# Down products of two MLPs by seven block products in place of eight, and a first projection that takes the weighted input

## The chip, the cores and the metric

The kernel runs on one core of a Trainium2 chip as a single program. Its engines work side by side, each through its own list of instructions in a fixed order: TensorE (PE, matmuls, with weight loads listed as PEld), VectorE (DVE), ScalarE (ACT), GpSimd (POOL) and SyncE (SP), which here issues most DMAs. They wait for one another by semaphores. The metric is the device time of one execution in microseconds.

## The reference

Two transformer blocks are computed on x of 1024 positions and 1024 features, in float32. Both end in the same kind of MLP, with 4096 inner features:

```
# block 1
u = rmsnorm(h, norm_mix);  proj = u @ w_in
h = h + concat(attention(proj), gated_deltanet(proj)) @ w_o
m = rmsnorm(h, norm_mlp)
h = h + square(relu(m @ w_up)) @ w_down
gate = sigmoid(rmsnorm(h, norm_ple) @ w_ple_gate)
h = h + gate * (p @ w_ple_proj)
x = rmsnorm(h, norm_final)
# block 2
u = rms_norm(x, norm_mix_2) @ w_in_2
x = x + concat(pool_mixer(u), hgrn2(u)) @ w_out_2
x = x + square(relu(rms_norm(x, norm_mlp_2) @ w_up_2)) @ w_down_2
return rms_norm(x, norm_final_2)
```

Attention is causal with a sliding window of 128 and rotary positions; the gated delta net and HGRN2 are recurrences over chunks of 64.

## The kernel before, in words

Activations are kept transposed: a tile holds 128 features by 512 positions (a half, h = 0 or 1). To keep float32 accuracy each operand is split into a high and a low part: a cast on ScalarE makes the high part (L203), a subtraction the low one (L204, mostly on VectorE). A product takes three matmuls per block of 128x128 weights: high by high (L223), high by low (L224), low by high (L225). Weight tiles are 128x1024; their parts are called wh and wl, those of activations u.

*The up product of an MLP* is done as a 2x2 block matrix product (feature tiles by halves) by seven block products in place of eight, after Strassen and Winograd. The operands made of the activations (b11, b21, and t1, t2, t3, b22, t4) are formed once, in the norm before it. For each of 16 pairs of inner feature tiles, n, the weight is read as four 128x512 tiles a11, a12, a21, a22 (L974, 256 KB each). Sums of these (s1 and s2 at L1006, L1007; two more at L1016, L1017) are split, and the products t2, t1, t3, b22, t4 follow, 12 matmuls each. VectorE adds each product to the running sums s and q as it ends (L1010, L1014, L1021, L1022, L1026, L1030). The products with b11 and b21 belong to the function `first`. For the first 12 n (HP) they are done ahead of the loop, from whole 512 KB tiles, and the partial sum goes through DRAM (p1s); for the last four they stand within the loop. A finished inner tile passes relu and square (L963, L964) and is put into the DRAM tensor `hid` (L965).

*The down product* is plain: for each half h and each half c4 of the output features four PSUM banks are filled over 8 groups g. A group takes two weight tiles of 512 KB and four tiles of `hid`, each split into high and low, and issues 48 matmuls. At the end of such a pass VectorE adds the four banks to the residual (L1055). Between the halves, `between` enters the norm of the first half of the result, to be worked off in small steps beside the matmuls (`tick`).

*The first projection* of block 1 (w_in) has two kinds of input. The attention's part takes xg, x times the norm's gain, and its results are multiplied by the reciprocal root Rs; the delta net's part takes u, x scaled fully (L281) and split. The rotary products run on GpSimd.

*What sets the order.* The kernel is written in a tile framework. It gives each engine one static order, by a scheduling of the whole program in which a tile is given its buffer when it is first written, and the buffers of one name come round in program order. In the up loop weight tiles and the results of sums draw their buffers from five such rings (x, y0, y1, y2, z) in a fixed sequence (`tq`). SP issues its DMAs in its static order: one that waits holds up those behind it.

Of the kernel before, what the change touches and what calls it, by code (L numbers as in the profile page):

```python
# [61 lines left out]
def block_kernel(ctx: ExitStack, tc: tile.TileContext, A):  # L62
# [186 lines left out]
    def rms(x, eps, r=None):  # L249


        a = tt("ac")
        SC.activation(a, x[0], ACTF.Square)
        for k in range(1, KD):
            sq = tt("sq")
            if r is not None and k % 2:
                G.tensor_tensor(sq, x[k], x[k], ALU.mult)
            else:
                SC.activation(sq, x[k], ACTF.Square)  # L259
            V.tensor_tensor(a, a, sq, ALU.add)  # L260
# [243 lines left out]
    res, hid = dram.tile([D, S], F32, name="res"), dram.tile([4 * D, S], F32, name="hid")  # L504
# [7 lines left out]
    xx, xg, u, Rs = [[], []], [[], []], [None, None], [None, None]  # L512
    r8 = const.tile([128, NC], F32, name="r8")

    def start(h):
        for k in range(KD):
            t = th(h, k)
            nc.sync.dma_start(out=t, in_=A["xT"][cs(k), hs(h)])
            xx[h].append(t)
            if h == 0 and k == KD - 1:  # L520
                early.append(load_w(A["w_in"][17]))
        for k in range(KD):
            hi, lo, g = tu(), tu(), small("norm_mix", k)
            SC.activation(hi, xx[h][k], ACTF.Copy, scale=g)
            V.scalar_tensor_tensor(lo, xx[h][k], g, hi.bitcast(F32), ALU.mult, ALU.subtract)
            xg[h].append((hi, lo))
        Rs[h] = td("b", 1 + h)
        SC.copy(Rs[h], value(rms(xx[h], 1e-6, r8[:, 4 * h:4 * h + 4])))
# [3 lines left out]
    start(0)  # L532
    early.insert(0, w)
# [31 lines left out]
    def attn_in():  # L565
        cosT, sinT = [td("a", 0), td("a", 1)], [td("a", 2), td("b", 0)]
        first = [td(r, 0) for r in "cdeg"] + [td("c", 1), td("d", 1)]
        dst = list(zip(first, [td(r, int(i)) for r, i in ("e1", "g1", "c2", "d2", "e2", "g2")]))

        def rope_in(h):  # L570
            for t, n in ((cosT, "cos"), (sinT, "sin")):
                nc.scalar.dma_start(out=t[h], in_=A[n][:, hs(h)])
                G.tensor_tensor(t[h], t[h], Rs[h], ALU.mult)

        def ev(i, h, ps):
            x = td("tmp", nxt(2, 3))
            SC.activation(x, ps, ACTF.Copy, scale=0.125 if i < 4 else 1.0)
            d = dst[i][h]
            if i < 5:
                t = tt("r")  # L580
                for q in range(0, 128, 32):
                    (nc.sync, nc.scalar)[q // 32 % 2].dma_start(out=t[q ^ 32:(q ^ 32) + 32, :], in_=x[q:q + 32, :])
                V.tensor_tensor(t, t, sinT[h], ALU.mult)
                G.tensor_tensor(x, x, cosT[h], ALU.mult)
                G.tensor_tensor(d, x, t, ALU.add)
            else:
                pp = axps()
                for c in range(4):
                    PE.transpose(pp[:, cs(c)], x[:, cs(c)], ident)
# [7 lines left out]
        rope_in(1)  # L597
        next(t)
        gates_in(0)
        u[0] = scaled(xx[0], small("norm_mix", 0, KD), Rs[0])  # L600
        run(t)
        gates_in(1)
        u[1] = scaled(xx[1], small("norm_mix", 0, KD), Rs[1])
        return dst[:4], dst[4], dst[5]
# [120 lines left out]
    def delta_in(j, h):  # L725
# [4 lines left out]
        def ev(i, h, ps):  # L730
            if i == 3:
                SC.activation(z, ps, ACTF.Sigmoid)
                V.tensor_tensor(z, ps, z, ALU.mult)
                return
            x = tx()
            tail = tails[:, (j * 3 + i) * 3:(j * 3 + i) * 3 + 3]
            SC.copy(x[:, 3:], ps)
# [13 lines left out]
        return (y, z), proj(u, [A["w_in"][4 * j + i] for i in range(4)], ev, (h,))  # L751
# [204 lines left out]
    def mlp(u, up, dn, between, before=None):  # L956
# [5 lines left out]
        def out(i, h, c):  # L962
            SC.activation(c, c, ACTF.Relu)  # L963
            SC.activation(c, c, ACTF.Square)  # L964
            nc.sync.dma_start(out=hid[cs(i), hs(h)], in_=c)  # L965
# [10 lines left out]

        def unit(*x):
            hi, lo = tl(pw, "wh", 3, 1024, F32R), tl(pw, "wl", 3, 1024, F32R)
# [4 lines left out]
        def first(w, s, c, n):  # L983
# [5 lines left out]
            out(2 * n, 0, c)  # L989
            tick()  # L990

        b11, b21 = u[0]
        for n in range(HP):
            s = tt("r")
            first(load_w(up[2 * n]), s, tt("f"), n)
            nc.sync.dma_start(out=p1s[cs(n), :], in_=s)
        x = u[1]
        for n in range(16):
            a11, a12, a21, a22 = [raw(up[2 * n + i][:, hs(k)]) for i in range(2) for k in range(2)]
            s = tt("ac")  # L1000
# [22 lines left out]
            out(2 * n + 1, 1, c)  # L1023
# [3 lines left out]
            out(2 * n, 1, q)  # L1027
# [49 lines left out]
    mlp(un, A["w_up"], A["w_down"], ug, ple_in)  # L1077
# [391 lines left out]
```

## Time and profile before

| | |
|---|---|
| median of 3 runs | 2587.14 us (2586.28 to 2589.57) |
| the profiled execution | 2584.28 us, its span 2582.2 us |
| mean granted clock of TensorE | 0.989 of full speed |
| busy: PE, DVE, ACT, POOL | 96%, 65%, 44%, 15% of the span |
| mean DMA traffic | 141 GB/s |
| up product of the first MLP; its down product and the gate | 601 to 907 us; 907 to 1285 us |
| the same of the second MLP, without a gate | 1896 to 2218 us; 2218 to 2582 us |

A row of the timeline gives the start of an instruction, its listed length, the engine, the line and the tiles as output<-inputs, and in brackets the engine's idle time before it with what released it. TensorE's matmuls are pipelined, so the distance of starts is their cost and not the listed length. PEclk is the granted clock as a share of 2.4 GHz.

### The profile page before, as it was taken

How to read it: one execution, taken by the hardware profiler on the slowest of the kernel's cores; microseconds unless marked ns; L12 is line 12 of the kernel's file. 1: busy time of each engine (PE TensorE's matmuls, PEld its weight loads, DVE VectorE, ACT ScalarE, POOL GpSimd, SP SyncE). 2: the span in 40 equal slices, each digit the busy share in tenths (PEclk: the TensorE clock that was granted, in tenths of full speed). 3: DMA queues.
4: the chain of work that ended last, by engine and by line, in shares of the span. 5: the costliest groups of instructions: out<-in, count | busy, mean ns of one | idle time of the engine just before them, and what ended most of it. 6: DMA issues, size and time to landing. Idle time of an engine off the chain costs nothing.

```text
span 2582.2 us, 41944 instructions
## 1 busy us (share of the span) xinstructions
PE 2489.7 (96%) x16150; PEld 2000.7 (77%) x16150; DVE 1677.1 (65%) x3065; ACT 1142.7 (44%) x1892; POOL 377.3 (15%) x430
## 2 busy tenths in 40 slices
PE   6999999999999999989999999999999999999997
PEld 4766777787888888878877778887778888888886
DVE  8787787869866565455457643446798665555653
ACT  4477444425545464344333332323455445544441
POOL 5611222200000000000022343344200000000000
PEclk8999999999999999999999999999999999999998
DMA  5311111354644376455422421113566443765662
GB/s 196 109 51 65 51 50 53 113 192 171 230 153 149 124 257 221 154 162 191 151 75 66 164 66 42 43 46 122 176 223 228 156 150 123 241 203 194 221 196 73
DMA packets 164585, 364.79 MB, mean 141 GB/s; under 512 B 18593, under 2 KB 23073, under 8 KB 164385
## 3 DMA queue, kind: packets, MB, share of 16 engines
q1 hardware_dynamic: 158960, 353.18, 41.4%
q10 hardware_dynamic: 5424, 8.94, 1.0%
q8 instruction: 126, 2.06, 0.3%
q14 instruction: 75, 0.61, 0.1%
HBM read 288.65 MB, written 70.78 MB: 139 GB/s over the span
## 4 chain that ended last, share of the span: by engine, by line
PE 79%; DVE 9%; issue 5%; POOL 3%; DMA 3%; ACT 1%; SPq 0%; DVEq 0%; ACTq 0%; POOLq 0%
PE m L223 13%; PE m L224 13%; PE m L225 13%; PE x L225 11%; PE x L223 11%; PE x L224 11%; DVE wl L204 1%; POOL u L204 1%; PE x L1235 1%; PE x L673 1%; DVE ac L260 1%; PE x L711 1%; DVE u L204 1%; DVE y L745 0%; PE x L702 0%
## 5 line engine op out<-in xcount | busy, mean ns | idle before, releaser
L223 PE MATMUL m<-u,wh 128*128 128x512 f32 x1676 | 673.4, 402 | 14.3 <-ACT wh L203 7.4
L224 PE MATMUL m<-u,wh 128*128 128x512 f32 x1676 | 664.1, 397 | 2.5 <-DVE u L204 1.8
L225 PE MATMUL m<-u,wl 128*128 128x512 f32 x1676 | 662.5, 395 | 2.5 <-DVE wl L204 2.4
L204 DVE TENSOR_TENSOR wl<-wr,wh 128x1024 fp32r<-128x1024 f32 (+2 forms) x277 | 343.1, 1239 | 296.1 <-ACT wh L203 284.6
L203 ACT CAST wh<-wr 128x1024 fp32r<-128x1024 f32 (+2 forms) x277 | 286.8, 1035 | 519.5 <-PE m L224 305.0
L223 PE MATMUL x<-u,wh 128*128 128x512 f32 x1012 | 395.2, 391 | 0.4 <-ACT u L203 0.4
L225 PE MATMUL x<-u,wl 128*128 128x512 f32 x1012 | 393.8, 390 | 1.5 <-DVE wl L204 1.5
L224 PE MATMUL x<-u,wh 128*128 128x512 f32 x1012 | 393.8, 389 | 0.0
L223 PEld LDWEIGHTS m<-u,wh 128*128 128x128 f32 x1676 | 316.4, 189 | 89.8 <-ACT wh L203 8.3
L224 PEld LDWEIGHTS m<-u,wh 128*128 128x128 f32 x1676 | 317.1, 189 | 72.4 <-issue 5.4
L225 PEld LDWEIGHTS m<-u,wl 128*128 128x128 f32 x1676 | 316.9, 189 | 71.1 <-DVE wl L204 4.3
L223 PEld LDWEIGHTS x<-u,wh 128*128 128x128 f32 x1012 | 190.4, 188 | 41.4 <-ACT u L203 1.3
L225 PEld LDWEIGHTS x<-u,wl 128*128 128x128 f32 x1012 | 190.0, 188 | 41.4 <-DVE wl L204 2.0
L224 PEld LDWEIGHTS x<-u,wh 128*128 128x128 f32 x1012 | 190.0, 188 | 40.5 <-issue 0.7
L203 ACT CAST u<-f 128x512 fp32r<-128x512 f32 x198 | 122.2, 620 | 196.0 <-PE x L224 72.2
L204 DVE TENSOR_TENSOR u<-f,u 128x512 fp32r<-128x512 f32 x174 | 123.1, 708 | 107.5 <-PE x L224 49.9
L204 POOL TENSOR_TENSOR u<-f,u 128x512 fp32r<-128x512 f32 x24 | 35.5, 1478 | 600.3 <-ACT u L203 599.5
L204 DVE TENSOR_TENSOR u<-r,u 128x512 fp32r<-128x512 f32 x128 | 88.1, 689 | 4.7 <-ACT u L203 4.5
L963 ACT ACTIVATE f<-f 128x512 f32<-128x512 f32 x56 | 35.4, 632 | 108.8 <-DVE f L1021 99.0
L203 ACT CAST u<-r 128x512 fp32r<-128x512 f32 x128 | 79.2, 618 | 9.1 <-DMA r<-hid 5.8
L203 ACT CAST wh<-y 128x512 fp32r<-128x512 f32 x86 | 51.8, 618 | 66.9 <-PE x L224 41.2
L260 DVE TENSOR_TENSOR ac<-ac,sq 128x512 f32<-128x512 f32 x70 | 53.9, 770 | 11.3 <-ACT sq L259 8.7
(748 smaller groups left out, 3608.8 us busy)
## 6 DMA issues: line engine op xcount, KB each, us to landing
wr<-in_w_down SPq DMA_DIRECT2D x128, 512.0 KB, 4.0
wr<-in_w_in SPq DMA_DIRECT2D x75, 512.0 KB, 3.4
r<-hid SPq DMA_DIRECT2D x128, 256.0 KB, 4.1
f<-hid SPq DMA_DIRECT2D x128, 256.0 KB, 3.3
y<-in_w_up SPq DMA_DIRECT2D x85, 256.0 KB, 3.3
hid<-f SPq DMA_DIRECT2D x56, 256.0 KB, 2.0
wr<-in_w_up SPq DMA_DIRECT2D x24, 512.0 KB, 3.9
hid<-sq SPq DMA_DIRECT2D x32, 256.0 KB, 2.7
```

What stands on the lines that cost most here:

```text
L203: SC.copy(hi, src)
L204: eng.tensor_tensor(lo, src, hi.bitcast(F32), ALU.subtract)
L223: PE.matmul(ps, whi[:, s], xh, start=(first and k == 0), stop=False)
L224: PE.matmul(ps, whi[:, s], xl, start=False, stop=False)
L225: PE.matmul(ps, wlo[:, s], xh, start=False, stop=(last and k == len(x) - 1))
L260: V.tensor_tensor(a, a, sq, ALU.add)
L673: PE.matmul(p3[kv][:, i], q[r, cs(n % 4)], kr[n // 4][r, (n % 4 - 1) * 128:(n % 4 + 1) * 128], start=True, stop=True)
L711: PE.matmul(po[r, 0:256], vT[m // 4][:, b:b + 64], pT[kv][:, q * 256:q * 256 + 256], start=(q == 0), stop=(q == nb - 1))
L963: SC.activation(c, c, ACTF.Relu)
L1235: PE.matmul(ps[p, c * 16:c * 16 + 16], k[:, m], odd(q[:, m], l), start=True, stop=True)
```

## The change

*Up loop.* The pairs of feature tiles are chosen in another way (`tiles`). The loop now also makes the operands of seven block products over the inner features: b11, b21, b22 are inner tiles, and t1 = b12 - b11, t2 = b22 - t1, t4 = t2 - b21, t3 = t2 - b11 are made by VectorE (L1053, L1062, L1064, L1066) and put into seven DRAM tensors, `hid[...]`. b12 of the first 12 n goes through DRAM (b12s). The sums of weights are made within 1024-wide tiles and split at once; t2, t3, t4 take their buffers from the same rings as the weight tiles.

*Down product.* Seven passes (t1, t2, b22, t3, b11, b21, t4) of 8 groups of 24 matmuls, with sums of weight blocks (s1, s2, s4, s3) made by VectorE from 256 KB loads. At the end of a pass the four banks are added to one to four sets of output tiles. `between` is called at the pass b21, and enters the input of the gate's projection too.

*Block 1.* All of the first projection takes xg, and each result is multiplied by Rs; the roots of a half are computed in a step of their own (`roots`). Rotary products move from GpSimd to VectorE, squares of the norm from GpSimd to ScalarE.

```diff
-            if r is not None and k % 2:
-                G.tensor_tensor(sq, x[k], x[k], ALU.mult)
-            else:
-                SC.activation(sq, x[k], ACTF.Square)
+            SC.activation(sq, x[k], ACTF.Square)
...
             xg[h].append((hi, lo))
-        Rs[h] = td("b", 1 + h)
-        SC.copy(Rs[h], value(rms(xx[h], 1e-6, r8[:, 4 * h:4 * h + 4])))
+
+    def roots(h):
+        r = value(rms(xx[h], 1e-6, r8[:, 4 * h:4 * h + 4]))
+        Rs[h] = tt("ac")
+        SC.copy(Rs[h], r)
...
     start(0)
+    roots(0)
...
         def rope_in(h):
             for t, n in ((cosT, "cos"), (sinT, "sin")):
                 nc.scalar.dma_start(out=t[h], in_=A[n][:, hs(h)])
-                G.tensor_tensor(t[h], t[h], Rs[h], ALU.mult)
+                V.tensor_tensor(t[h], t[h], Rs[h], ALU.mult)
...
+                V.scalar_tensor_tensor(d, ps, scale, cosT[h], ALU.mult, ALU.mult)
                 V.tensor_tensor(t, t, sinT[h], ALU.mult)
-                G.tensor_tensor(x, x, cosT[h], ALU.mult)
-                G.tensor_tensor(d, x, t, ALU.add)
+                V.tensor_tensor(d, d, t, ALU.add)
...
-        u[0] = scaled(xx[0], small("norm_mix", 0, KD), Rs[0])
+        roots(1)
+        rope_in(1)
         run(t)
         gates_in(1)
-        u[1] = scaled(xx[1], small("norm_mix", 0, KD), Rs[1])
         return dst[:4], dst[4], dst[5]
...
             if i == 3:
-                SC.activation(z, ps, ACTF.Sigmoid)
-                V.tensor_tensor(z, ps, z, ALU.mult)
+                V.tensor_tensor(z, ps, Rs[h], ALU.mult)
+                r = tt("r")
+                SC.activation(r, z, ACTF.Sigmoid)
+                V.tensor_tensor(z, z, r, ALU.mult)
...
-            SC.copy(x[:, 3:], ps)
+            V.tensor_tensor(x[:, 3:], ps, Rs[h], ALU.mult)
...
 
-        def out(i, h, c):
+        def relu2(c):
             SC.activation(c, c, ACTF.Relu)
             SC.activation(c, c, ACTF.Square)
-            nc.sync.dma_start(out=hid[cs(i), hs(h)], in_=c)
+
+        def put(name, n, t):
+            nc.sync.dma_start(out=hid[name][cs(n), :], in_=t)
 
...
-            hi, lo = tl(pw, "wh", 3, 1024, F32R), tl(pw, "wl", 3, 1024, F32R)
+            hi, lo = hilo()
             for i, t in enumerate(x):
                 split(t, hi[:, hs(i)], lo[:, hs(i)])
             return hi, lo
 
-        def first(w, s, c, n):
+        def first(w, s, c):
             p = product(w, 0, b11)
             SC.copy(s, p)
             tick()
             p = product(w, 1, b21)
             V.tensor_tensor(c, p, s, ALU.add)
-            out(2 * n, 0, c)
+            relu2(c)
             tick()
+
+        def tiles(n):
+            t = 4 * (n // 2) + n % 2
+            return t, t + 2
 
         b11, b21 = u[0]
         for n in range(HP):
-            s = tt("r")
-            first(load_w(up[2 * n]), s, tt("f"), n)
+            s, c = tt("r"), tt("f")
+            first(load_w(up[tiles(n)[0]]), s, c)
             nc.sync.dma_start(out=p1s[cs(n), :], in_=s)
+            nc.sync.dma_start(out=b12s[cs(n), :], in_=c)
         x = u[1]
         for n in range(16):
-            a11, a12, a21, a22 = [raw(up[2 * n + i][:, hs(k)]) for i in range(2) for k in range(2)]
-            s = tt("ac")
+            a11, a12, a21, a22 = [raw(up[t][:, hs(k)]) for t in tiles(n) for k in range(2)]
+            s, c12 = tt("ac"), tt("r")
             if n < HP:
                 nc.sync.dma_start(out=s, in_=p1s[cs(n), :])
+                nc.sync.dma_start(out=c12, in_=b12s[cs(n), :])
             else:
-                first(unit(a11, a12), s, tt("r"), n)
-            s1, s2 = tq(), tq()
+                first(unit(a11, a12), s, c12)
+            w2 = tl(pw, "wr", 2, 1024)
+            s2, s1 = w2[:, hs(0)], w2[:, hs(1)]
             V.tensor_tensor(s1, a21, a22, ALU.add)
             V.tensor_tensor(s2, s1, a11, ALU.subtract)
-            w = unit(s2, s1)
+            w = hilo()
+            split(w2, *w)
             p = product(w, 0, x["t2"])
             V.tensor_tensor(s, p, s, ALU.add)
             tick()
@@ -1013,49 +1034,121 @@
             q = tt("sq")
             V.tensor_tensor(q, p, s, ALU.add)
             tick()
-            V.tensor_tensor(a21, a11, a21, ALU.subtract)
-            V.tensor_tensor(a12, a12, s2, ALU.subtract)
-            w = unit(a21, a12)
+            w3 = tl(pw, "wr", 2, 1024)
+            V.tensor_tensor(w3[:, hs(0)], a11, a21, ALU.subtract)
+            V.tensor_tensor(w3[:, hs(1)], a12, s2, ALU.subtract)
+            w = hilo()
+            split(w3, *w)
             p = product(w, 0, x["t3"])
             c = tt("f")
             V.tensor_tensor(c, p, q, ALU.add)
             V.tensor_tensor(s, p, s, ALU.add)
...
             p = product(w, 1, x["b22"])
             V.tensor_tensor(q, p, q, ALU.add)
-            out(2 * n, 1, q)
+            relu2(q)
+            put("b11", n, q)
+            V.tensor_tensor(c12, c12, q, ALU.subtract)
+            put("t1", n, c12)
             tick()
             p = product(unit(a22), 0, x["t4"])
             V.tensor_tensor(s, s, p, ALU.subtract)
-            out(2 * n + 1, 0, s)
+            relu2(s)
+            put("b22", n, s)
+
+            t2, t3, t4 = tq(), tq(), tq()
+            V.tensor_tensor(t2, s, c12, ALU.subtract)
+            put("t2", n, t2)
+            V.tensor_tensor(t4, t2, c, ALU.subtract)
+            put("t4", n, t4)
+            V.tensor_tensor(t3, t2, q, ALU.subtract)
+            put("t3", n, t3)
             tick()
 
-        for h in range(2):
-            for c4 in range(2):
-                if before is not None and (h, c4) == (1, 1):
-                    before()
-                banks = [pps() for _ in range(4)]
-                for g in range(8):
-                    ws = [load_w(dn[4 * g + 2 * c4 + i]) for i in range(2)]
-                    x = []
-                    for k in range(4):
-                        f = tt("fr"[k % 2])
-                        nc.sync.dma_start(out=f, in_=hid[cs(4 * g + k), hs(h)])
-                        hi, lo = tu(), tu()
-                        split(f, hi, lo)
-                        x.append((hi, lo))
-                    for i in range(4):
-                        acc(banks[i], ws[i // 2], i % 2 * H, x, g == 0, g == 7)
-                        tick()
+        def block(i, j, g, c):
+
+            return dn[4 * g + 2 * i + c].rearrange("p (m k n) -> p m k n", m=2, k=4)[:, :, 2 * j:2 * j + 2]
+
+        def v4(t):
+            return t.rearrange("p (m k n) -> p m k n", m=2, k=2)
+
+        def block2(i, j, g):
+            t = tl(pw, "wr", 2, 1024)
+            for c in range(2):
+                nc.sync.dma_start(out=v4(t[:, hs(c)]), in_=block(i, j, g, c))
+            return t
+
+        kept = [[None, None] for _ in range(8)]
+
+        def s1(g):
+            w = block2(1, 1, g)
+            for c in range(2):
+                t = kept[g][c] = tr()
+                nc.sync.dma_start(out=v4(t), in_=block(1, 0, g, c))
+                V.tensor_tensor(t, t, w[:, hs(c)], ALU.add)
+            return unit(*kept[g])
+
+        def s2(g):
+            w = block2(0, 0, g)
+            for c, t in enumerate(kept[g]):
+                V.tensor_tensor(t, t, w[:, hs(c)], ALU.subtract)
+            return unit(*kept[g])
+
+        def s4(g):
+            w = block2(0, 1, g)
+            for c, t in enumerate(kept[g]):
+                V.tensor_tensor(t, w[:, hs(c)], t, ALU.subtract)
+            return unit(*kept[g])
+
+        def s3(g):
+            w, ts = block2(0, 0, g), [tr(), tr()]
+            for c, t in enumerate(ts):
+                nc.sync.dma_start(out=v4(t), in_=block(1, 0, g, c))
+                V.tensor_tensor(t, w[:, hs(c)], t, ALU.subtract)
+            return unit(*ts)
+
+        def plain(i, j):
+            def f(g):
+                w = hilo()
+                split(block2(i, j, g), *w)
+                return w
+            return f
+
+        begun = set()
+
+        C = {"C12": (0, 0), "C22": (0, 4), "C11": (1, 0), "C21": (1, 4)}
+        for f, name, to in ((s1, "t1", ("C12", "C22")), (s2, "t2", ("C12", "C22", "C21")), (s4, "b22", ("C12",)),
+                            (s3, "t3", ("C22", "C21")), (plain(0, 0), "b11", ("C12", "C22", "C21", "C11")),
+                            (plain(0, 1), "b21", ("C11",)), (plain(1, 1), "t4", ("C21",))):
+            if name == "b21":
+                between()
+            banks = [pps() for _ in range(4)]
+            for g in range(8):
+                w = f(g)
+                x = []
+                for k in range(2):
+                    t = tt("fr"[k])
+                    nc.sync.dma_start(out=t, in_=hid[name][cs(2 * g + k), :])
+                    hi, lo = tu(), tu()
+                    split(t, hi, lo)
+                    x.append((hi, lo))
                 for i in range(4):
-                    m = 4 * c4 + i
-                    t = th(h, m)
-                    nc.sync.dma_start(out=t, in_=res[cs(m), hs(h)])
-                    V.tensor_tensor(t, banks[i], t, ALU.add)
-                    hh[h][m] = t
-            if h == 0:
-                between()
+                    acc(banks[i], w, i * 256, x, g == 0, g == 7)
+                    tick()
+            for i in range(4):
+                for o in to:
+                    h, m = C[o][0], C[o][1] + i
+                    if o not in begun:
+                        hh[h][m] = th(h, m)
+                        nc.sync.dma_start(out=hh[h][m], in_=res[cs(m), hs(h)])
+                    t = hh[h][m]
+                    if name == "t4":
+                        V.tensor_tensor(t, t, banks[i], ALU.subtract)
+                    else:
+                        V.tensor_tensor(t, banks[i], t, ALU.add)
+            begun.update(to)
```

**The order in the up loop of the first MLP.** On VectorE before, from the end of one feature tile into the next: L1026 and L1030 close the tile whose sums are sq_7632 and ac_7593, L1010 and L1014 open the next (ac_7707, sq_7746), and L1006, L1007, L1016 make weight sums.

```order
L1022 TENSOR_TENSOR ac_7593<-x0_7642,ac_7593 128x512
L1026 TENSOR_TENSOR sq_7632<-x1_7661,sq_7632 128x512
L204 TENSOR_TENSOR wl_7751<-y2_7703,wh_7750 128x512
L204 TENSOR_TENSOR wl_7751<-x_7701,wh_7750 128x512
L1030 TENSOR_TENSOR ac_7593<-ac_7593,x1_7682 128x512
L204 TENSOR_TENSOR wl_7793<-z_7705,wh_7792 128x512
L1010 TENSOR_TENSOR ac_7707<-m_7719,ac_7707 128x512
L1006 TENSOR_TENSOR y0_8051<-y2_8045,z_8047 128x512
L1007 TENSOR_TENSOR x_8052<-y0_8051,y1_8041 128x512
L1016 TENSOR_TENSOR y2_8045<-y1_8041,y2_8045 128x512
L1014 TENSOR_TENSOR sq_7746<-m_7733,ac_7707 128x512
```

On VectorE now, from the end of the first tile into the next: L1057 closes it (ac_7520); L1062, L1064 and L1066 make operands of the down product; L1026 to L1039 are weight sums and the wl rows splits; L1031 takes the next tile's first product (m_7654).

```order
L1057 TENSOR_TENSOR ac_7520<-ac_7520,x1_7609 128x512
L1062 TENSOR_TENSOR z_7626<-ac_7520,r_7521 128x512
L1064 TENSOR_TENSOR y1_7628<-z_7626,f_7580 128x512
L1066 TENSOR_TENSOR y0_7627<-z_7626,sq_7558 128x512
L1026 TENSOR_TENSOR wr_7647<-z_7639,y0_7641 128x512
L1038 TENSOR_TENSOR wr_7683<-x_7635,z_7639 128x512
L1027 TENSOR_TENSOR wr_7647<-wr_7647,x_7635 128x512
L1039 TENSOR_TENSOR wr_7683<-y2_7637,wr_7647 128x512
L204 TENSOR_TENSOR wl_7651<-wr_7647,wh_7650 128x1024
L204 TENSOR_TENSOR wl_7687<-wr_7683,wh_7686 128x1024
L204 TENSOR_TENSOR wl_7729<-y0_7641,wh_7728 128x512
L1031 TENSOR_TENSOR ac_7643<-m_7654,ac_7643 128x512
```

The sums L1006, L1007 and L1016 before belong to a tile two further on, and the next tile's products follow without them; now the sums and splits of the very next tile stand between the last operand and L1031.

On SP before, puts of inner tiles (L965), loads of weight tiles (L974) and of the partial sum (L1002) in the same loop:

```order
L965 DMA hid_98<-ac_7821 128x512
L1002 DMA ac_8049<-p1s_99 128x512
L974 DMA x_8385<-in_w_up 128x512
L965 DMA hid_98<-f_7997 128x512
L974 DMA y2_8387<-in_w_up 128x512
L965 DMA hid_98<-sq_7974 128x512
L974 DMA z_8389<-in_w_up 128x512
L965 DMA hid_98<-ac_7935 128x512
L974 DMA y0_8503<-in_w_up 128x512
L1002 DMA ac_8163<-p1s_99 128x512
```

On SP now, the seven puts of the first tile (L975), then loads of weight tiles (L984) and of a partial sum (L1020):

```order
L975 DMA hid_b21_99<-f_7580 128x512
L975 DMA hid_b11_98<-sq_7558 128x512
L975 DMA hid_t1_101<-r_7521 128x512
L975 DMA hid_b22_100<-ac_7520 128x512
L975 DMA hid_t2_102<-z_7626 128x512
L975 DMA hid_t4_104<-y1_7628 128x512
L975 DMA hid_t3_103<-y0_7627 128x512
L984 DMA z_7639<-in_w_up 128x512
L984 DMA y0_7641<-in_w_up 128x512
L984 DMA y0_7760<-in_w_up 128x512
L1020 DMA ac_7766<-p1s_106 128x512
```

Loads stood singly between the puts; now z_7639 and y0_7641, which L1026 reads above, stand behind the last of the puts, that of t3 (y0_7627).

On VectorE now, at the start of the pass b21 of the first MLP: the scaled tiles of the first half's norm (L278) and their splits; u_11830, from f_11827, is an operand of the pass's second group.

```order
L278 SCALAR_TENSOR_TENSOR f_11766<-x_10034,smalls_88,x2_11758 128x512
L204 TENSOR_TENSOR u_11763<-f_11760,u_11762 128x512
L278 SCALAR_TENSOR_TENSOR f_11772<-x_10040,smalls_88,x2_11758 128x512
L278 SCALAR_TENSOR_TENSOR f_11778<-y0_10046,smalls_88,x2_11758 128x512
L204 TENSOR_TENSOR u_11775<-f_11772,u_11774 128x512
L278 SCALAR_TENSOR_TENSOR f_11784<-z_10031,smalls_88,x2_11758 128x512
L278 SCALAR_TENSOR_TENSOR f_11790<-y1_10037,smalls_88,x2_11758 128x512
L204 TENSOR_TENSOR u_11787<-f_11784,u_11786 128x512
L278 SCALAR_TENSOR_TENSOR f_11796<-y2_10043,smalls_88,x2_11758 128x512
L278 SCALAR_TENSOR_TENSOR f_11802<-y1_10049,smalls_88,x2_11758 128x512
L204 TENSOR_TENSOR u_11799<-f_11796,u_11798 128x512
L204 TENSOR_TENSOR u_11830<-f_11827,u_11829 128x512
```

The operands of the second group come behind all of the norm's scaled tiles.

## Rows read from the trace of the kernel before

**Rows 1.** The page, busy us of each engine, share, instructions.

```profile
PE 2489.7 (96%) x16150; PEld 2000.7 (77%) x16150; DVE 1677.1 (65%) x3065; ACT 1142.7 (44%) x1892; POOL 377.3 (15%) x430
```

**Rows 2.** Busy time by stage: stage, length, engines (instructions), clock, DMA share, GB/s.

```profile
0.00:123.00 123.00, 98.88 (x416) 73.07 (x417) 98.56 (x136) 55.71 (x86) 76.25 (x60) 0.94 0.47 151
...
601.00:907.00 306.00, 302.90 (x1339) 249.70 (x1339) 221.26 (x351) 160.82 (x268) 0.00 (x0) 1.00 0.49 165
...
1896.00:2218.00 322.00, 318.88 (x1405) 261.64 (x1404) 231.20 (x363) 170.26 (x284) 0.00 (x0) 1.00 0.52 172
```

**Rows 3.** The page, groups: busy, mean ns of one, idle before and releaser.

```profile
L223 PE MATMUL m<-u,wh 128*128 128x512 f32 x1676 | 673.4, 402 | 14.3 <-ACT wh L203 7.4
...
L204 DVE TENSOR_TENSOR wl<-wr,wh 128x1024 fp32r<-128x1024 f32 (+2 forms) x277 | 343.1, 1239 | 296.1 <-ACT wh L203 284.6
L203 ACT CAST wh<-wr 128x1024 fp32r<-128x1024 f32 (+2 forms) x277 | 286.8, 1035 | 519.5 <-PE m L224 305.0
```

**Rows 4.** Timeline of TensorE in the up loop: start, length, engine, line, operation.

```profile
764.50 0.39 PE L225 MATMUL m<-tmp,wl 128*128 128x512 f32 x1
764.73 0.39 PE L223 MATMUL m<-u,wh 128*128 128x512 f32 x1
...
765.86 0.39 PE L225 MATMUL m<-u,wl 128*128 128x512 f32 x1
```

**Rows 5.** Timeline of VectorE in the same stretch, with the idle time before.

```profile
764.93 0.69 DVE L1030 TENSOR_TENSOR ac<-ac,m 128x512 f32<-128x512 f32 x1 [0.83 <-PE m L225]
...
769.75 0.69 DVE L1006 TENSOR_TENSOR z<-y,x 128x512 f32<-128x512 f32 x1 [1.41 <-DMA x<-in_w_up]
770.48 0.69 DVE L1007 TENSOR_TENSOR y<-z,y 128x512 f32<-128x512 f32 x1
771.09 0.69 DVE L1016 TENSOR_TENSOR y<-y,y 128x512 f32<-128x512 f32 x1
```

**Rows 6.** Timeline of ScalarE in the same stretch.

```profile
765.65 0.63 ACT L963 ACTIVATE ac<-ac 128x512 f32<-128x512 f32 x1 [0.32 <-DVE ac L1030]
766.31 0.63 ACT L964 ACTIVATE ac<-ac 128x512 f32<-128x512 f32 x1
```

**Rows 7.** Timeline of the DMA issues of SyncE in the same stretch.

```profile
764.34 0.38 SPq L965 DMA_DIRECT2D hid<-sq  x1
764.82 0.38 SPq L974 DMA_DIRECT2D y<-in_w_up  x1
766.24 0.33 SPq L974 DMA_DIRECT2D x<-in_w_up  x1
766.97 0.33 SPq L965 DMA_DIRECT2D hid<-ac  x1
```

**Rows 8.** The page, DMA issues: count, KB each, median us to landing.

```profile
y<-in_w_up SPq DMA_DIRECT2D x85, 256.0 KB, 3.3
```

**Rows 9.** Timeline of TensorE behind the norm of the first half, first MLP.

```profile
1117.28 0.80 PE L223 MATMUL x<-a,c 128*128 128x512 f32 x1 [5.19 <-DVE f L281]
1117.87 0.63 PE L224 MATMUL x<-a,c 128*128 128x512 f32 x1
1118.30 0.63 PE L225 MATMUL x<-a,c 128*128 128x512 f32 x1
...
1121.41 0.79 PE L223 MATMUL m<-u,wh 128*128 128x512 f32 x1 [1.21 <-ACT u L203]
...
1125.39 0.39 PE L223 MATMUL m<-u,wh 128*128 128x512 f32 x1
```

**Rows 10.** Waits of TensorE from 0 to 130 us: total, times, longest.

```profile
PE x L244 <- DVE ac L260: 11.5, 2, 10.4
```

**Rows 11.** Timeline of VectorE in that norm: last sum, first scaled tiles.

```profile
1099.90 0.69 DVE L260 TENSOR_TENSOR ac<-ac,sq 128x512 f32<-128x512 f32 x1
...
1105.96 1.41 DVE L281 SCALAR_TENSOR_TENSOR f<-x,smalls,x 128x512 f32<-128x512 f32 x2
```

**Rows 12.** Busy time by stretch, columns as in Rows 2.

```profile
10.00:20.00 10.00, 8.42 (x28) 5.46 (x27) 9.81 (x13) 6.42 (x10) 7.63 (x9) 1.00 1.02 377
```

More of the change, by code (lines that the diff above doesn't have):

```diff
@@ L503, in block_kernel @@
     xs, hm = dram.tile([D, S], F32, name="xs"), dram.tile([D, S], F32, name="hm")
-    res, hid = dram.tile([D, S], F32, name="res"), dram.tile([4 * D, S], F32, name="hid")
+    res = dram.tile([D, S], F32, name="res")
+    hid = {n: dram.tile([2 * D, H], F32, name=f"hid_{n}") for n in ("b11", "b21", "b22", "t1", "t2", "t3", "t4")}
+    b12s = dram.tile([HP * 128, H], F32, name="b12s")
     p1s = dram.tile([HP * 128, H], F32, name="p1s")
@@ L509, in block_kernel @@
     mix = mix_new("mix1")
-    xx, xg, u, Rs = [[], []], [[], []], [None, None], [None, None]
+    xx, xg, Rs = [[], []], [[], []], [None, None]
     r8 = const.tile([128, NC], F32, name="r8")
@@ L572, in rope_in @@
                 nc.scalar.dma_start(out=t[h], in_=A[n][:, hs(h)])
-                G.tensor_tensor(t[h], t[h], Rs[h], ALU.mult)
+                V.tensor_tensor(t[h], t[h], Rs[h], ALU.mult)
         def ev(i, h, ps):
-            x = td("tmp", nxt(2, 3))
-            SC.activation(x, ps, ACTF.Copy, scale=0.125 if i < 4 else 1.0)
+            x, scale = td("tmp", nxt(2, 3)), 0.125 if i < 4 else 1.0
+            SC.activation(x, ps, ACTF.Copy, scale=scale)
             d = dst[i][h]
@@ L596, in attn_in @@
         start(1)
-        rope_in(1)
         next(t)
         gates_in(0)
-        u[0] = scaled(xx[0], small("norm_mix", 0, KD), Rs[0])
+        roots(1)
+        rope_in(1)
         run(t)
         gates_in(1)
-        u[1] = scaled(xx[1], small("norm_mix", 0, KD), Rs[1])
         return dst[:4], dst[4], dst[5]
@@ L749, in ev @@
             y.append(t)
-        return (y, z), proj(u, [A["w_in"][4 * j + i] for i in range(4)], ev, (h,))
+        return (y, z), proj(xg, [A["w_in"][4 * j + i] for i in range(4)], ev, (h,))
     states = {}
@@ L953, in block_kernel, with mlp @@
     un()
-    def mlp(u, up, dn, between, before=None):
+    def mlp(u, up, dn, between):
         side[0] = 2
-        def out(i, h, c):
+        def relu2(c):
             SC.activation(c, c, ACTF.Relu)
             SC.activation(c, c, ACTF.Square)
-            nc.sync.dma_start(out=hid[cs(i), hs(h)], in_=c)
+        def put(name, n, t):
+            nc.sync.dma_start(out=hid[name][cs(n), :], in_=t)
         def product(w, i, x):
@@ L975, in raw, with hilo @@
             return t
+        def hilo():
+            return tl(pw, "wh", 3, 1024, F32R), tl(pw, "wl", 3, 1024, F32R)
         def unit(*x):
-            hi, lo = tl(pw, "wh", 3, 1024, F32R), tl(pw, "wl", 3, 1024, F32R)
+            hi, lo = hilo()
             for i, t in enumerate(x):
@@ L1022, in mlp @@
             V.tensor_tensor(s, p, s, ALU.add)
-            out(2 * n + 1, 1, c)
+            relu2(c)
+            put("b21", n, c)
             tick()
@@ L1076, in block_kernel, with second @@
     ug = norm("norm_ple", 1e-6)
-    mlp(un, A["w_up"], A["w_down"], ug, ple_in)
+    def second():
+        ug()
+        ple_in()
+    mlp(un, A["w_up"], A["w_down"], second)
     ug()
```

## The prediction

> **What bounds the kernel now.** I read the busy times first [rows 1]: TensorE is busy 2489.7 of 2582.2 us, VectorE 1677, GpSimd 377. The table by stage [rows 2] says where it is not: 24.1 us are idle in the first 123 us, while in the two stages that hold most of the up products (601 to 907, 1896 to 2218) TensorE is busy 302.90 of 306.00 and 318.88 of 322.00. So matmul count sets the time there, as long as operands arrive. The timeline of TensorE gives the price of one 128x512 matmul at full clock: starts 0.23 us apart (764.50, 764.73; the six steps from 764.50 to 765.86 give 0.2267 on the mean, [rows 4]), though each is listed with 0.39, and with 402 ns in its group [rows 3]. VectorE has room in the up loop, about 70% busy [rows 2], so it is the order of its work and not the sum that I follow below.
>
> **What is removed.** A down product of 4 passes x 8 groups x 48 matmuls becomes 7 x 8 x 24, that is 1536 to 1344 in each MLP: 2 x 192 x 0.2267 = **-87.1 us**, all of it on the engine that bounds.
>
> **What is added to the up loop.** Per feature tile n: three more sums (L1062, L1064, L1066) and L1053, seven puts for four. At 0.61 us each, start to start [rows 5], the four cost VectorE 2.4 us of a 13.6 us period (60 matmuls x 0.2267), and before it idles some 4 us of that; by amount they are hidden. By place they are not. In the order of VectorE the weight sums and splits of tile n+1 (L1026 to L1039, wl) now stand behind L1066 of n; before, such sums stood two tiles ahead of their use. In the order of SP the loads of a21 and a22 of n+1 (L984) stand behind the put of t3, which waits for L1066. TensorE has the t2 product of n+1 straight behind t4 of n, with nothing between for n+1 = 1 to 11 (for 12 to 15 the 24 matmuls of b11 and b21 stand between). So a chain runs in every tile that ran beside TensorE before. With T the moment after the last t4 matmul:
> - L1057 starts at T+0.20, as L1030 did (764.73 in [rows 4], 764.93 in [rows 5]).
> - Relu starts 0.72 later (765.65), square 0.66 behind (766.31) and takes 0.63 [rows 6]; its put was issued at 766.97 [rows 7]. L1062 starts at T+2.24.
> - L1064 depends on it: +0.73 (769.75 to 770.48); L1066: +0.61 (770.48 to 771.09) and 0.69 long [rows 5]. t3 stands at T+4.27.
> - The put of t3 and two loads are issued at 0.33 to 0.48 each [rows 7]: a22 goes out at T+5.15.
> - A load lands 3.3 us later (median, [rows 8]; the load of 766.24 in [rows 7] released L1006 at 769.75, 3.5 us). L1026 at T+8.45.
> - L1038, L1027: +0.6 each, and 0.69: the pair w2 is whole at T+10.35. Its cast takes 1.04 [rows 3]: TensorE begins at **T+11.5**. Its third matmul needs wl, 1.24 behind the cast [rows 3]: T+12.7.
> - After 5.19 us without work the granted clock was at its lower level, 1.2 GHz: starts 0.43 apart (1117.87, 1118.30), and it was at 2.4 GHz again 4.0 us after TensorE resumed at 1121.41 (first row of 0.39 at 1125.39, [rows 9]). I take the same here: up to T+15.5, so the t2 product ends at T+16.3 and not at T+2.7. The four other products take 48 x 0.2267 = 10.9.
>
> The period is 27.2 us for 13.6, or for 12 to 15 27.2 for 19.0: 11 x 13.6 + 4 x 8.2 = 182 per MLP, **+365 us** in all.
>
> A rule that weighs on this: the Trainium skill, "TensorE: Matmul & The Clock Gate", section "HAM oscillation — how this bites in real kernels", says that a loop whose matmuls are shorter than the wait for its next operand falls back to the slow clock in every step, and pays for it each time. The trace shows one such fall behind one wait [rows 9], none in a loop. By the rule all 30 gaps are cold, which is what the sum has; were none, t2 would end 1.35 us earlier and the total be 40 us less.
>
> The skill's "DMA: Bandwidth & Descriptors", section "Anatomy of one DMA", has a DMA cost about 2.0 us plus its bytes at 436 GB/s; an estimate from that page is 2.6 us for 256 KB, 0.7 under the row's 3.3, and the total would be 21 us less by it. The row decides.
>
> **What is added to the down passes.** Per group VectorE has 2 weight sums, 2 operand splits and two 512-wide or one 1024-wide weight split, 6 x 0.61 = 3.7 of 5.44 us (24 x 0.2267): hidden. Loads are 1.5 MB per group in the passes t1 and t3, that is 276 to 289 GB/s; 377 was seen [rows 12], so nothing, though the runs of 1 KB are new and nothing shows them: at 250 GB/s it would be 0.6 x 8 x 4 = +18, and I keep that as the upper end. At the ends of the passes 8, 12, 4, 8, 16, 4 and 4 sums of 0.61 stand for four times 4. At t1 to t2 the last bank's two, a weight sum and two splits stand ahead of the third matmul: about 3 us, and 1 at the start of t1, +8 for both MLPs (0 to 20). At b11 to b21 of the first MLP the norm of the first half follows: 16 sums (first at the first bank's end, 4 us before the pass ends at E) to E+5.8, 7 sums of L257 and two splits 7.4; from the last of these to the first scaled tile 6.1 (1099.90 to 1105.96, [rows 11]); eight L278 and four splits 8.4: E+27 until VectorE makes the operand of the pass's second group. Before it TensorE has one group (5.44), 12 matmuls (2.7) and the norm's own: 17 idle and 2.5 cold, against 5.19 + 1.21 idle and some 2.6 cold now [rows 9]. I take **+15** with the 4 added (9 to 23); the second MLP has its operands split ahead of it and adds nothing.
>
> **Block 1.** The 16 scalings and 16 splits of u go, the rope's products go from GpSimd to VectorE. TensorE's idle time here is led by one wait of 10.4 us for the sum of squares (L260, [rows 10]) while GpSimd is busy 76 of 123 us [rows 2]; the start splits this norm off. It can't give more than the 24.1 idle, and VectorE, busy 98.56 of 123 [rows 2], takes some 24 x 0.7 = 17 us more: -24 to +10, I take the wait's size, **-10**.
>
> **The sum.** 2584.28 (the profiled execution: span 2582.2 and 2.1 around it, which stays) - 87.1 + 365 + 8 + 15 - 10 = 2875; the median of the runs stands 2.9 above that execution: **2878 us**. Its own range: the clock back twice as late after each gap +1.85 x 30 = +55, the loads 0.8 slower +24, against -40 and -21 above: 2800 to 2960.
>
> **Rivals.**
> 1. The loads are not what is late: the queue issues them in time and VectorE's order alone binds. Then L1026 starts at T+4.2, TensorE at T+7.25, the period is 22.9, 9.3 x 11 + 3.9 x 4 = 118 per MLP, 237 in all: **2750**. For it: such loads ran well ahead before. Against: their place behind a put that waits.
> 2. The other side: TensorE stays fed in the up loop, and the saving stands: -87.1 + 8 + 15 - 10 = -74, **2513**. It takes the chain of 11.5 us to lie beside other matmuls. It decides below 74 / 30 = 2.5 us of gap per tile. For it: TensorE waited hardly at all in this loop, with VectorE at the same share [rows 2]. Against: nothing stands between t4 and t2, and relu, square and three sums alone are over 4 us.
> 3. The clock stays at the low level through both up loops, since TensorE is idle two fifths of each period: all 60 matmuls at 0.427, period 37.4, +23.8 x 11 + 18.4 x 4 = 335 per MLP: about **3180**. For it: only the slope of rows 9; against: 16 us of unbroken matmuls in each period, where 4.0 brought it back.
>
> **Chances.** The forecast 0.76, rival 1 0.09, rival 2 0.10, rival 3 0.03; 0.02 for gaps that eat the saving just so. Range for 8 in 10: 2740 to 2960. Within 0.2% (about 5 us, what a measurement of this kernel tells from none): 0.01. Faster 0.10, slower 0.89.
>
> **What would show it.** In the trace after: in the up loops TensorE idle some 11 us before each first t2 matmul, released by ACT's cast wh, with the row before that VectorE's L1026 waiting for DMA of in_w_up; the period 27 us; clock at half behind each. A period of 23 with L1026 unwaiting is rival 1, one near 14 rival 2. In the down passes 5.44 us per group, a gap of some 17 us a group into the b21 pass of MLP 1 alone. Wrong would be: PE busy throughout the up loops, or down groups well over 5.44.

## The result, and the profile after

The median is 2910.44 us (2903.34 to 2915.41, 4 runs) against 2587.82 for the kernel before: a ratio of 1.124, 95% interval 1.122 to 1.126. 2878 was forecast. By landmarks in the two traces (first sum of an up product, last L1030 or L1057, last sum of a down product):

| stage | before, us | after, us | change | forecast |
|---|---|---|---|---|
| to the first up product | 625.5 | 616.9 | -8.6 | -10 |
| up product, MLP 1 | 297.7 | 499.7 | +202.0 | +182 |
| down product, MLP 1 | 363.6 | 337.6 | -26.0 | -24.5 |
| between | 627.4 | 628.6 | +1.2 | 0 |
| up product, MLP 2 | 300.8 | 496.6 | +195.8 | +182 |
| down product, MLP 2 | 350.2 | 309.8 | -40.4 | -39.5 |
| end | 17.0 | 17.0 | 0 | 0 |

(A down product's forecast is -43.55 for its 192 matmuls, with +4 for the starts of t1 and t2, and +15 in the first MLP.) Busy time by these stages, columns as in [rows 2]: in the kernel before for the two products of the first MLP, then in the kernel after for the two up and the two down products:

```profile
625.50:923.20 297.70, 297.36 (x1312) 245.82 (x1311) 209.05 (x324) 158.06 (x265) 0.00 (x0) 1.00 0.51 170
923.20:1286.80 363.60, 356.53 (x1558) 292.47 (x1557) 196.29 (x253) 159.25 (x222) 5.38 (x4) 0.99 0.59 190
```

```profile
616.90:1116.60 499.70, 340.08 (x1321) 266.75 (x1320) 249.59 (x353) 154.23 (x231) 0.00 (x0) 0.83 0.39 134
1116.60:1454.20 337.60, 313.88 (x1364) 255.74 (x1364) 237.99 (x366) 144.42 (x231) 5.08 (x4) 0.97 0.66 213
...
2082.80:2579.40 496.60, 338.35 (x1330) 265.55 (x1330) 253.11 (x366) 154.46 (x231) 0.00 (x0) 0.83 0.38 133
2579.40:2889.20 309.80, 306.95 (x1352) 251.43 (x1350) 226.04 (x353) 132.86 (x212) 0.00 (x0) 1.00 0.69 227
```

In the up products TensorE is now idle for a third, VectorE is busy for only half of the time and GpSimd not at all: no engine is the bound, a chain is. The waits of TensorE name its last link (total, times, longest), in the up product of the first MLP and in that of the second:

```profile
PE x L223 <- ACT wh L203: 121.5, 12, 12.7
PE m L223 <- ACT wh L203: 35.7, 3, 12.2
...
PE x L223 <- ACT wh L203: 99.7, 9, 12.7
PE m L223 <- ACT wh L203: 56.8, 6, 11.7
```

30 waits of 314 us in all are for a cast of weights; before, the whole group of L223 m had 14.3 us idle in the whole program [rows 3]. One gap of the kernel after, VectorE first (T, the start of the last t4 matmul, 832.12, and one step of 0.23, is 832.35):

```profile
832.54 0.69 DVE L1057 TENSOR_TENSOR ac<-ac,m 128x512 f32<-128x512 f32 x1
834.59 0.69 DVE L1062 TENSOR_TENSOR x<-ac,r 128x512 f32<-128x512 f32 x1 [1.36 <-ACT ac L972]
835.31 0.69 DVE L1064 TENSOR_TENSOR y<-x,f 128x512 f32<-128x512 f32 x1
835.92 0.69 DVE L1066 TENSOR_TENSOR z<-x,sq 128x512 f32<-128x512 f32 x1
840.98 0.69 DVE L1026 TENSOR_TENSOR wr<-y,z 128x512 f32<-128x512 f32 x1 [4.37 <-DMA z<-in_w_up]
841.59 0.68 DVE L1038 TENSOR_TENSOR wr<-y,y 128x512 f32<-128x512 f32 x1
842.19 0.68 DVE L1027 TENSOR_TENSOR wr<-wr,y 128x512 f32<-128x512 f32 x1
```

The issues of SyncE in the same gap:

```profile
836.63 0.32 SPq L975 DMA_DIRECT2D hid_t<-z  x1
837.01 0.45 SPq L984 DMA_DIRECT2D x<-in_w_up  x1
837.51 1.40 SPq L984 DMA_DIRECT2D z<-in_w_up  x3
```

And TensorE ahead of this gap and behind it:

```profile
815.36 0.80 PE L223 MATMUL x<-u,wh 128*128 128x512 f32 x1 [12.58 <-ACT wh L203]
...
821.48 0.59 PE L224 MATMUL x<-u,wh 128*128 128x512 f32 x1
821.90 0.40 PE L225 MATMUL x<-u,wl 128*128 128x512 f32 x1
...
832.12 0.39 PE L225 MATMUL m<-tmp,wl 128*128 128x512 f32 x1
844.06 0.79 PE L223 MATMUL m<-u,wh 128*128 128x512 f32 x1 [11.55 <-ACT wh L203]
```

Read it from the top: L1066 ends at T+4.26, the put of t3 goes out at T+4.28, the loads right behind it, VectorE is idle for 4.37 us until the second has landed, and TensorE resumes at T+11.71. The period is 28.70 us (815.36 to 844.06).

### The profile page after: what moved, and what is told of

It is laid out like the page before. It is cut to its first block, busy times and chain, and to the rows that moved or that the text cites. A ratio compares the mean times of both kernels' runs of the same rounds, so it can differ in the third digit from the quotient of the medians.

```text
span 2906.2 us, 41653 instructions
## 1 busy us (share of the span) xinstructions
PE 2485.8 (86%) x15766; PEld 1966.4 (68%) x15766; DVE 1831.2 (63%) x3385; ACT 1088.3 (37%) x1810; POOL 309.7 (11%) x390
## 4 chain that ended last, share of the span: by engine, by line
PE 64%; DVE 13%; issue 9%; DMA 9%; ACT 3%; POOL 2%; SPq 1%; POOLq 0%; ACTq 0%; DVEq 0%
PE m L223 11%; PE m L225 11%; PE m L224 11%; PE x L223 8%; PE x L225 7%; PE x L224 7%; DMA y<-in_w_up 2%; ACT wh L203 2%; DMA z<-in_w_up 1%; DVE wl L204 1%; DMA wr<-in_w_down 1%; DVE u L204 1%; DMA f<-hid_t 1%; PE x L714 1%; DVE ac L1057 1%
## 5 line engine op out<-in xcount | busy, mean ns | idle before, releaser
L223 PE MATMUL m<-u,wh 128*128 128x512 f32 x1628 | 665.9, 410 | 110.6 <-ACT wh L203 102.7
L224 PE MATMUL m<-u,wh 128*128 128x512 f32 x1628 | 653.8, 402 | 3.0 <-DVE u L204 2.9
L223 PE MATMUL x<-u,wh 128*128 128x512 f32 x932 | 384.3, 413 | 225.1 <-ACT wh L203 223.4
L203 ACT CAST wh<-wr 128x1024 fp32r<-128x1024 f32 (+2 forms) x261 | 266.5, 1032 | 636.5 <-PE m L224 290.9
L223 PEld LDWEIGHTS m<-u,wh 128*128 128x128 f32 x1628 | 313.1, 193 | 190.6 <-ACT wh L203 112.3
L204 DVE TENSOR_TENSOR wl<-wr,wh 128x1024 fp32r<-128x1024 f32 (+2 forms) x261 | 315.5, 1218 | 170.6 <-ACT wh L203 160.4
L225 PE MATMUL x<-u,wl 128*128 128x512 f32 x932 | 380.1, 409 | 2.2 <-DVE wl L204 1.5
L224 PE MATMUL x<-u,wh 128*128 128x512 f32 x932 | 378.9, 407 | 1.1 <-DVE u L204 1.1
L223 PEld LDWEIGHTS x<-u,wh 128*128 128x128 f32 x932 | 185.7, 199 | 273.3 <-ACT wh L203 232.7
L203 ACT CAST u<-f 128x512 fp32r<-128x512 f32 x166 | 102.5, 620 | 196.1 <-PE x L224 66.2
L204 DVE TENSOR_TENSOR u<-f,u 128x512 fp32r<-128x512 f32 x150 | 103.7, 692 | 71.0 <-ACT u L203 66.4
L204 POOL TENSOR_TENSOR u<-f,u 128x512 fp32r<-128x512 f32 x16 | 22.4, 1399 | 850.6 <-ACT u L203 849.8
L204 DVE TENSOR_TENSOR u<-r,u 128x512 fp32r<-128x512 f32 x112 | 76.7, 685 | 8.2 <-ACT u L203 8.2
L750 DVE SCALAR_TENSOR_TENSOR y<-x,smalls,y 128x512 f32<-128x512 f32 x72 | 57.0, 796 | 2.6 <-ACT y L748 2.4
```

The lines of the kernel that those rows point to most:

```text
L203: SC.copy(hi, src)
L204: eng.tensor_tensor(lo, src, hi.bitcast(F32), ALU.subtract)
L223: PE.matmul(ps, whi[:, s], xh, start=(first and k == 0), stop=False)
L224: PE.matmul(ps, whi[:, s], xl, start=False, stop=False)
L225: PE.matmul(ps, wlo[:, s], xh, start=False, stop=(last and k == len(x) - 1))
L750: V.scalar_tensor_tensor(t, x[:, 3 - s:3 - s + H], cw(3 - s), t, ALU.mult, ALU.add)
```

## The experiments

**In place.** The operands t2, t4, t3 are written over b12, b21, b11.

```diff
-            t2, t3, t4 = tq(), tq(), tq()
-            V.tensor_tensor(t2, s, c12, ALU.subtract)
-            put("t2", n, t2)
+            V.tensor_tensor(c12, s, c12, ALU.subtract)
+            put("t2", n, c12)
...
```

> Only the places of t2, t4 and t3 change: they are written over b12, b21 and b11 (whose puts have gone out) and draw no buffer from the rings of the weight tiles. The same sums, puts and loads are made; the order now has the weight sums and splits of the next tile ahead of L1057 and its loads two tiles ahead. Theory (the loads and weight sums of the next tile stand behind t3, by the rings): the gaps of 11 to 12 us before each t2 product go, the up stages fall back to about the 298 and 301 us of the kernel before, and the time is 2908 - 398 = about 2510. Rival (VectorE's added sums, or the added puts and loads on the queue, are themselves the cost): the gaps stay in size or spread, the up stages stay above 400 us each, 2700 to 2900.

Measured: 2518.62 us; ratio to before 0.974 (0.9725 to 0.9754). The two up products take 300.6 and 303.3 us (297.7 and 300.8 before), with as many sums and puts as in the change; the first of them:

```profile
617.00:917.60 300.60, 299.42 (x1320) 247.11 (x1318) 244.31 (x353) 155.56 (x231) 0.00 (x0) 1.00 0.67 229
```

VectorE in the same loop, where L1057 ends a tile and L1038 and L1039 are weight sums of the next:

```profile
797.92 0.68 DVE L1038 TENSOR_TENSOR wr<-z,y 128x512 f32<-128x512 f32 x1
798.52 0.68 DVE L1057 TENSOR_TENSOR ac<-ac,x 128x512 f32<-128x512 f32 x1
...
799.72 0.69 DVE L1039 TENSOR_TENSOR wr<-y,wr 128x512 f32<-128x512 f32 x1
```

VectorE is busy for 244 of 301 us and TensorE for 299: the added work fits beside the matmuls. The rival falls; all but 5.4 of the 398 us are the price of the places and not of the work. A ring of their own for t2, t4 and t3, which would tell the sharing of the ring from the new buffers as such, was not tried.

**Loads on another queue.**

```diff
             t = tq()
-            nc.sync.dma_start(out=t, in_=src)
+            nc.gpsimd.dma_start(out=t, in_=src)
```

> Only the queue of the loads of a11, a12, a21, a22 changes, from SyncE's to GpSimd's, which has little to do there; VectorE's order in the up loop stays as it is, with the weight sums behind t3. The loads then no longer wait behind the put of t3. Theory (both the queue and VectorE's order hold the product back, the queue by 4.4 us a tile, the rest by order): VectorE's L1026 follows L1066 without idle time, TensorE resumes about 7.2 us after the last t4 matmul and not 11.7, and 30 x 4.4 = 130 us go: about 2775. Rival 1 (the queue is all of it): the gaps go and the time is about 2515. Rival 2 (the place behind the put costs nothing; the loads are late for want of bandwidth or buffers): within 15 us of 2908.

Measured: 2780.88 us, ratio 1.0755 (1.0739 to 1.0771). VectorE in one gap of it, and TensorE behind:

```profile
762.60 0.68 DVE L1066 TENSOR_TENSOR y<-x,sq 128x512 f32<-128x512 f32 x1
763.20 0.68 DVE L1026 TENSOR_TENSOR wr<-y,z 128x512 f32<-128x512 f32 x1
```

```profile
742.43 0.79 PE L223 MATMUL x<-u,wh 128*128 128x512 f32 x1 [7.10 <-ACT wh L203]
...
758.80 0.39 PE L225 MATMUL x<-tmp,wl 128*128 128x512 f32 x1
766.28 0.80 PE L223 MATMUL x<-u,wh 128*128 128x512 f32 x1 [7.09 <-ACT wh L203]
```

L1026 now follows L1066 without a wait, the gap is 7.1 us and the period 23.85. This is the chain of the first rival of the prediction (7.25, 22.9; 2750), made by hand: the place of the loads is worth 130 us, VectorE's order the other 262 (2780.88 to 2518.62).

**Block 1 alone**, the kernel before with the new first projection (roots in a step of their own, results multiplied by Rs, rotary products on VectorE, and the norm's squares on ScalarE).

```diff
-        u[0] = scaled(xx[0], small("norm_mix", 0, KD), Rs[0])
+        roots(1)
+        rope_in(1)
...
```

> The kernel before with the change of block 1's first projection alone; both MLPs as before. Theory: 625.5 to 616.9 us at the first sum of the up product, so 8 to 9 us faster than before, 2579, and nothing else moves. Rival (the start is worth nothing by itself and the 8.6 us come from how the rest of the program was ordered): within 3 us of 2587.

Measured: 2576.07 against 2585.74 us, ratio 0.9960 (0.9946 to 0.9975): faster by 9.7. In the trace of the full change the wait of 10.4 us [rows 10] is gone; the largest left from 0 to 130 us is for the first casts of weights (7.4 before), and the first 123 us read

```profile
PE m L223 <- ACT wh L203: 8.1, 2, 7.2
```

```profile
0.00:123.00 123.00, 106.22 (x445) 78.76 (x446) 81.27 (x159) 55.88 (x84) 7.03 (x22) 0.94 0.48 155
```

with 106 us of TensorE for 99, GpSimd down from 76 to 7, and VectorE busy for less with more instructions [rows 2].

**Filled gaps.**

```diff
+            warm = unit(a22)
...
+            if n < 11:
+                idle = pps()
+                for k in range(46):
+                    PE.matmul(idle, warm[0][:, cs(k % 4)], b11[k % 4][0], start=k == 0, stop=k == 45)
```

> The changed kernel with 46 more matmuls (46 x 0.2267 = 10.4 us) behind the t4 product of the feature tiles 0 to 10 of both MLPs, into a bank that nobody reads; they lie in the gaps of 11.3 to 12.7 us and delay nothing. Theory (each gap costs twice, by its length and by the lower clock behind it, where the trace shows 13 to 15 starts 0.43 apart): the clock stays at its upper level, the t2 product ends 2.5 us earlier, less the wait for wl, and 22 x 2.5 = 55 us go: about 2855. Rival (the lower clock behind a gap costs next to nothing, as wl is late there anyway): 2900 to 2910. Rival 2 (the added matmuls reach past the gap): slower than 2910.

Measured: 2871.25 us, ratio to before 1.1104 (1.1085 to 1.1122), so 39 us less than the change alone, with 1012 matmuls more. Behind a filled gap:

```profile
700.62 0.50 PE L223 MATMUL m<-u,wh 128*128 128x512 f32 x1 [1.27 <-ACT wh L203]
700.96 0.40 PE L224 MATMUL m<-u,wh 128*128 128x512 f32 x1
701.20 0.39 PE L223 MATMUL x<-u,wh 128*128 128x512 f32 x1
```

The next starts are 0.34 and 0.24 apart, and not 0.43 to 0.67: the clock had stayed up. It gives 1.8 us a gap and not 2.5: in 7 of the 22 filled gaps, where some idle time was left, the clock fell none the less, as here:

```profile
836.15 0.80 PE L223 MATMUL m<-u,wh 128*128 128x512 f32 x1 [2.75 <-ACT wh L203]
836.75 0.63 PE L224 MATMUL m<-u,wh 128*128 128x512 f32 x1
```

In this kernel's order matmuls of another product (into x in the rows above) also stand ahead of the first with wl, so part of the gain may be the wait for wl, 0.24 us behind the change's gap at 701.61 (starts 0.67 apart for 0.43). That the lower clock is a cost of its own, beside the idle time, is shown by the rest; its size is some 1.5 to 1.8 us on the mean of these gaps. The expectation's 13 to 15 starts at the lower clock hold in 8 of the change's 30 gaps; the others have 7 to 11, so 2.5 us a gap was too much.

**A later norm**, on top of the operands in place.

```diff
-            if name == "b21":
-                between()
             banks = [pps() for _ in range(4)]
             for g in range(8):
+                if name == "b21" and g == 4:
+                    between()
```

> As the first of these, and the norm between the halves is entered behind the fourth group of the pass b21 and not before its first, so that VectorE makes the operands of four groups before the norm's. Theory (the gap of some 20 us and the cold clock behind it come from one prefetched group in front of a chain of 27 us): 17 to 22 us less than the first, about 2490. Rival (the norm's result is what the next stage waits for, so the wait moves to the gate's projection): within 5 us of the first.

Measured: 2504.86 us, ratio 0.9687 (0.9671 to 0.9704): 13.8 less than in place, short of 17. Of the 20 us of idle time at this place 11.5 are left, most of it at the gate's projection, where the rival had it:

```profile
1178.23 0.80 PE L223 MATMUL x<-d,g 128*128 128x512 f32 x1 [9.46 <-DVE f L278]
1183.16 0.50 PE L223 MATMUL m<-u,wh 128*128 128x512 f32 x1 [2.00 <-ACT u L203]
```

**Another bank for the gate's projection**, on top of that.

```diff
-        p2_ = axps()
+        p2_ = axps(i % 2)
```

> As the kernel with the late norm, and the gate's projection of the first block takes its PSUM banks from x0 and x1 in turn; before, its first two products drew x2, stood in TensorE's order right behind the norm's broadcast (L270), which lies in x2, and had to wait until VectorE had read that for its eight scaled tiles. Theory (it is this bank that holds up TensorE for 9.46 us in that kernel, with 2.0 us for operands behind it and the clock's 2 to 3 us): 9 to 13 us less than 2505, about 2494. Rival (TensorE would wait as long for the operands of the fifth group, which VectorE makes behind the norm): within 4 us of 2505.

Measured: 2496.74 us (2493.7 to 2503.33), ratio 0.9656 (0.9638 to 0.9674); the intervals of the two overlap, so it is not settled whether this edit gains. Its profiled execution, the longest of its runs, shows where the wait went:

```profile
1185.25 0.80 PE L223 MATMUL m<-u,wh 128*128 128x512 f32 x1 [14.74 <-ACT u L203]
```

In this execution the bank was not the bound: TensorE waits even longer, 14.74 us for 9.46 and 2.00, for the operands of the next group, as the rival said. Two of the four runs took less than 2494 us, as the theory said; no trace shows them. In this trace ScalarE's cast of these operands waits for their load, which draws its buffer from the ring f, as the norm's scaled tiles before it do:

```profile
1184.58 0.62 ACT L203 CAST u<-f 128x512 fp32r<-128x512 f32 x1 [2.63 <-DMA f<-hid_b]
```

That this ring, and the ring of the u, are the cause was not tried.

## Why the prediction came out as it did

- **The chain in the up loop** is the one described, step for step: L1062 at T+2.24 (forecast 2.24), L1066's end at T+4.26 (4.27), the put of t3 at T+4.28, L1026 at T+8.63 (8.45), TensorE at T+11.71 (11.5). Both links were taken apart on the chip, the queue (130 us) and VectorE's order (262 us). In four of the last eight gaps the wait stands ahead of the product with b11 and not of t2, as the loads of its weights are behind the same put; the gaps there are as long.
- **The term that was too small** is that of the up loops, 365 for 398. By the forecast the gaps sum to 22 x 11.3 + 8 x 5.9 = 296 us; the 30 waits are 314. Behind the gaps 365 - 296 = 69 were forecast for the lower clock and wl, and 398 - 314 = 84 came. So the idle time was 18 us short, 0.6 a gap, and the rest 15. The idle time is that of the loads: in 21 of the 22 longer gaps L1026 waits for one and starts at T+9.1 on the mean, for 8.45; loads from w_up into y land in a median of 4.0 us, for 3.3 in [rows 8]:

```profile
y<-in_w_up SPq DMA_DIRECT2D x72, 256.0 KB, 4.0
```

  Why they take longer was not traced. In this kernel up to four loads and two of partial sums go out at once behind the put, which was not so in the trace from which 3.3 was taken. The estimate of 2.6 us from the Trainium skill's "DMA: Bandwidth & Descriptors", section "Anatomy of one DMA", was farther off still; the Trainium skill gives that fit for DMAs of the gpsimd path, and these loads are issued by SyncE.
- **The clock.** The Trainium skill ("TensorE: Matmul & The Clock Gate", section "HAM oscillation — how this bites in real kernels") has a loop pay for the slow clock in every step when its matmuls are shorter than the wait for the next operand. Here they are longer, 13.6 us at full clock for a wait of 12, so the prediction stretched that rule; the trace shows the fall all the same. Behind each of the 30 waits 7 to 14 matmuls start at the lower level, and 0.83 is the mean granted clock in both up products. The clock was back 3.4 to 6.5 us after TensorE resumed (4.3 at 701.61, 6.5 at 815.36), 4.7 on the mean, where I had taken 4.0 for all: at half speed that is an estimated 30 x 0.35 = 10 of the 15 us. The 4.0 was counted from 1121.41, but in [rows 9] TensorE had worked from 1117.28, with 1.21 us idle between; that it came near the mean is luck.
- **Block 1** came to -8.6 us (-9.7 alone) for -10, in part by luck: the size was taken from one wait. That wait went, but VectorE, which was to take 17 us more, was busy for 17 us less (98.56 to 81.27).
- **The down products** were right, -26.0 and -40.4 us: VectorE's 3.7 us and the loads of 1 KB runs lie beside the 5.44 us of matmuls. The DMA share was 1.04 in the pass t1 and 0.72 in t3, and TensorE was busy for 41 and 43 of 44 us:

```profile
1113.00:1157.00 44.00, 41.25 (x178) 32.68 (x177) 33.65 (x53) 20.79 (x36) 0.00 (x0) 1.00 1.04 350
...
1247.00:1291.00 44.00, 43.29 (x192) 35.56 (x191) 32.88 (x53) 24.46 (x43) 0.00 (x0) 1.00 0.72 225
```

- **The norm at b21** had the right size (17 idle and 2.5 cold forecast, 20 us idle found), by a description that left something out. I had TensorE wait once, for the operands of the second group. It waits in three places before that, for the norm's own matmuls and for the gate's projection, which stand ahead in its order:

```profile
1352.34 0.66 PE L244 MATMUL x<-ac,ones 128*32 128x128 f32 x8 [8.22 <-DVE ac L257]
1356.53 2.07 PE L270 MATMUL x<-ac,ones 128*128 128x512 f32 x2 [3.53 <-DVE ac L267]
1368.43 0.80 PE L223 MATMUL x<-d,g 128*128 128x512 f32 x1 [7.27 <-DVE f L278]
1372.29 0.50 PE L223 MATMUL m<-u,wh 128*128 128x512 f32 x1 [0.93 <-ACT u L203]
```

  As all of it ends with the same chain of VectorE, the sum is the same; in the profiled execution of the last experiment, taking away one of these waits only handed the time to the next.
- **The rivals.** The first (VectorE's order alone) is what is left when the loads are early, not what the change does. The second, the fast side, holds for the same arithmetic with operands in place, 2518.62 for 2513. The third (the clock stays low) did not come: in every period of the up loops the matmuls were back at 0.23 us a start.

## What to carry to other kernels

A saving on the engine that bounds counts only as long as its next operand is made beside it: where a new tile is drawn from a ring that also holds the next step's loads, a static order puts these loads and all that hangs on them behind the new tile. Here a change that takes 87 us of matmuls away added 398 us to the up products. Look at what stands between the last product of one step and the first of the next on every engine, the DMA queue included; writing results over tiles that are done with kept the saving here. The later norm and the other bank bring the time to about 2500, the fastest versions of this study.

## What the runs showed of the hardware

The lower clock outlasts a gap by differing times in one and the same loop: 4.3 us at 701.61 and 6.5 us at 815.36, after 12.0 and 12.6 us of idle time (3.4 to 6.5 over its 30 gaps), and 5.7 us at 742.43 after 7.1 in the kernel with loads on the other queue. One value from one gap is not enough to price thirty. DMA traffic of 350 GB/s, two thirds of it by the program in runs of 1 KB, stood beside matmuls in the pass t1 without holding them up by more than 3 us in 44.
